# Score mask and first bias table loaded during the first value projection, half of the first pair's key copies on VectorE, the exponential's table loaded ahead

## The chip, the cores and the metric

The kernel runs on one core of a Trainium2 chip. The metric is the device time of one execution in microseconds (us). TensorE (PE) does the matrix products, VectorE (DVE), ScalarE (ACT) and GpSimd (POOL) the elementwise work, and SyncE (SP) and ScalarE issue the transfers. Each engine takes its instructions in the order in which they were put on it. A transfer issued by ScalarE stands in the same order as ScalarE's arithmetic: if its target buffer is still being read, ScalarE stands still with it.

## The reference

One step of a two-layer diffusion trunk on 512 latent tokens (a grid of 8 rows of 64) and 128 context tokens, width 1024. Only the first layer's token mixer matters here:

```python
q, k, v = jnp.split(h @ w_qkv, 3, axis=-1)          # 16 heads of 64
s_lat = einsum(qg, kg) * scale                      # each latent reads an 8 x 16 neighbourhood
bias  = rpb[:, dr, dc]                              # learned bias by relative row and column
s_lat = where(col_ok, s_lat + bias, -inf)
s_ctx = einsum(qg, k_ctx) * scale                   # and all 128 cached context keys
p = softmax(concatenate([s_lat, s_ctx]))
o = einsum(p_lat, vg) + einsum(p_ctx, v_ctx)
```

Here `h` is the RMS-normalized input, scaled and shifted by a modulation computed from the conditioning vector. The second layer (grouped-query attention) and both feed-forward blocks follow and are untouched.

## The kernel before

The kernel keeps fp32 accuracy by splitting each operand into a rounded high part (`wh`, `kh`, `hT[0]`) and a low part (`wl`, `kl`, `hT[1]`): a cast on ScalarE makes the high part, a subtraction on VectorE or GpSimd the low part, and `passes` runs three products.

The order on TensorE is written out: `mm` and `turn` chain every product and transpose to the one before. The order on the other engines is made ahead of the run by a planner: it takes the instructions in program order as priority, gives each a modelled time, and starts whatever is ready first. `behind(a, b)` adds nothing at run time; it only forces `a` after `b` in the order of their engine.

What happens around the change, in order of time:

- **First values** (lines 583 to 649). The input is normalized and transposed to `xT`. The modulation comes in four quarters: `mod_rows(i)` multiplies, ScalarE copies `row` to `rs`, `mod_cols(i)` turns it into columns, and ScalarE and VectorE write two of the eight blocks of `hT`. `normed` holds the last ScalarE and the last VectorE instruction of it. Between the quarters TensorE runs `v_part(k, ...)`, block `k` of the value projection of heads 0 to 3. Two small tables `cr` for the feed-forward convolution are loaded through ScalarE's queue and transposed on TensorE (`cp`) after `v_part(5)`. At the end `na_v_put` copies the values out of PSUM.
- **Pairs of heads.** `na_qk_items(p)` yields the work for heads 2p and 2p+1: eight parts for queries, eight for keys, each in two column halves. After a query half ScalarE and VectorE write `qs` (lines 841, 842); after a key half `k_put` (811 to 816) copies keys for both heads: for each head `b` ScalarE writes the head's own 64 partitions (814), then the same source rows into the other 64 partitions (815), and VectorE makes `kl` (816). The cached context keys go through `tk` the same way.
- **Score tables.** `na_table(h)` (883 to 896) loads runs of head h's bias into `tr` (one buffer, three transfers on ScalarE's queue, line 887) and GpSimd subtracts them from `mask` into `tb` (three instructions of 128x256, line 892). `tb` alternates between two buffers. The mask itself is loaded at line 760.
- **Heads.** `fill(PRO)` runs the first 20 parts: queries and keys of pair 0 and the first half of the queries of pair 1. Then `Head(0)` makes its table, and `scores(slot)` runs for four slots with one part (`f`) between them: two products into `s`, VectorE adds the table and takes the minimum (927), ScalarE takes the exponential (931), VectorE the reciprocal (934), GpSimd scales (935). `ORDER0` then interleaves parts, transposes `t0`..`t2` of the probabilities and the scores of the next head.

Weights come through SP's queue into four `wr` buffers well ahead of their use.

Of the kernel before, what the change touches and what calls it, by code (L numbers as in the profile page):

```python
# [10 lines left out]
F32 = mybir.dt.float32  # L11
F32R = mybir.dt.float32r
BF16 = mybir.dt.bfloat16
AF = mybir.ActivationFunctionType
# [5 lines left out]
P = 128  # L20
# [14 lines left out]
RPAD = 32  # L35
# [36 lines left out]
def raw_ap(ap, offset, dims):  # L72
    return bass.AP(tensor=ap.tensor, offset=ap.offset + offset, ap=[list(d) for d in dims])
# [30 lines left out]
def hybrid_step(ctx: ExitStack, tc: tile.TileContext, A, O):  # L104
    nc = tc.nc
# [3 lines left out]
    def pe(ins):  # L109

        if pe_last[0] is not None:
            tc.add_manual_dep(ins.ins, pe_last[0], no_sync, reason="order")
        pe_last[0] = ins.ins.name
# [3 lines left out]

    def turn(*a, **k):
        pe(nc.tensor.transpose(*a, **k))  # L119

    def f32(t):
        return t.bitcast(F32)

    def pool(name, bufs=1, side="left", **k):
        return tc.tile_pool(name=name, bufs=bufs, side=side, reuse_waits="tile", **k)
# [336 lines left out]
    hT = new_hT(r_h0.enter_context(pool("h0", 1, "right")))  # L462
    l_na = ExitStack()
    vpool = l_na.enter_context(pool("nav", 3))
    wqkv = A["na_w_qkv"][0]

    def na_v_tile():
        return vpool.tile([P, 6, 4, HD], F32, tag="vt", name="vt", bufs=2)

    def na_v_put(vt, c, src):  # L470
        nc.scalar.copy(vt[:, c], src.rearrange("p (a d) -> p a d", a=4))

    def na_v_cache(vts, g):
        vc = vpool.tile([P, 256], F32, tag="vc", name="vc", bufs=1)
# [13 lines left out]
    with ExitStack() as s:  # L488
# [57 lines left out]
        def mod_rows(i, ws):  # L546


            row = bk.get("row")
            for (n, h), w in ws.items():  # L550
                for j in range(4):
                    k = 4 * h + j
                    mm(row[32 * j : 32 * j + 32, 256 * n : 256 * n + 256], scolp[:, 2 * k : 2 * k + 32],
                       w[:, j, :], start=h == 0, stop=h == 1)
            rs = sp.tile([P, 512], F32, tag="rs", name="rs")
            nc.scalar.copy(rs, row)
            bk.put(row)
            return rs
# [46 lines left out]
        def v_part(k, cs):  # L605
            for c in cs:
                wh, wl = wv[k // 4]
                passes(vb[c][:, 0:256], tuple(x[:, k, c * P : c * P + P] for x in hT),
                       (wh[:, k % 4, :], wl[:, k % 4, :]), k == 0, k == KC - 1)
# [12 lines left out]
        mod_cols(2, rs)  # L622
        v_part(2, range(3, NT))
        v_part(3, range(NT))
        rs = mod_rows(3, loads[3])
        v_part(4, range(3))
        mod_cols(3, rs)
# [15 lines left out]
        v_part(6, range(NT))  # L643
        for c in range(NT):
            v_part(7, (c,))
            na_v_put(vts_of[0], c, vb[c][:, 0:256])
            if c == 4:
                na_v_out(0, vb[c][:, 0:256])
            bk.put(vb[c])

# [49 lines left out]
            nc.scalar.copy(hi, raw)  # L702
            return nc.vector.tensor_sub(lo, raw, f32(hi))

    def behind(ins, other):
        tc.add_manual_dep(ins.ins, other.ins.name, no_sync, reason="order")

    class Mix:


# [45 lines left out]

    with l_na:
        ap = l_na.enter_context(pool("na", 2))
        mask = ap.tile([P, 2, 32, 8], F32, name="mask", bufs=1)
        nc.scalar.dma_start(mask, A["k_mask"])  # L760
        tbs = [ap.tile([P, 7, P], F32, name=f"tb{i}", bufs=1) for i in range(2)]
        for tb in tbs:
            nc.gpsimd.memset(tb[:, 3, :], 0.0)
# [1 line left out]
        for i in range(2):  # L765
            for b in range(2):
                nc.gpsimd.memset(f32(kls[i][b])[own_oth(b)[1], :], 0.0)
        qk_of = {}

        def na_v_items(g):  # L770
            d = {}
# [25 lines left out]
        def na_qk_items(p):  # L797
            d = {}

            def load_q():  # L800
                d["w"] = wsplit(rows(wqkv, 0, 8, P * p, P), 8, P, nc.gpsimd if p else None, after=None if p else normed)
                kc = ap.tile([P, P], F32, tag="kc", name="kc", bufs=2)
                nc.scalar.dma_start(
                    kc, A["cache_na_k"][0, 0][:, 2 * p : 2 * p + 2, :].rearrange("t h d -> t (h d)")
                )
                d["kc"] = kc

            def load_k():
                d["wk"] = wsplit(rows(wqkv, 0, 8, 1024 + P * p, P), 8, P, nc.gpsimd if p else None)

            def k_put(c0, c1, src):
                for b in range(2):
                    own, oth = own_oth(b)
                    nc.scalar.copy(d["kh"][b][own, c0:c1], src[own])
                    nc.scalar.copy(d["kh"][b][oth, c0:c1], src[own])
                    nc.vector.tensor_sub(d["kl"][b][own, c0:c1], src[own], f32(d["kh"][b][own, c0:c1]))

            def part(which, half, k0):
                w = d["w"] if which == 0 else d["wk"]
                cs = QKH[half]  # L820
                nq = cs.stop - cs.start
                if k0 == 0:
                    d["ps"] = bk.get("qk")
                pp = d["ps"]
                for k in (k0, k0 + 1):
                    for n, (hx, wx) in enumerate(((0, 0), (0, 1), (1, 0))):
                        mm(pp[:, 0:nq], w[wx][:, k, :], hT[hx][:, k, cs],
                           start=k == 0 and n == 0, stop=k == 7 and n == 2)
                if k0 < 6:
                    return  # L830
                if which == 0:
                    if half == 0:
                        d["qs"] = [ap.tile([P, QW], F32R, tag=f"qs{b}", name=f"qs{b}") for b in range(2)]
                    pieces = [(slice(64 + cs.start, 64 + cs.stop), slice(0, nq))]
                    if half == 1:
                        pieces.append((slice(0, 64), slice(NS - 64 - cs.start, NS - cs.start)))
                    for qc, pc in pieces:
                        for b in range(2):
                            own, oth = own_oth(b)
                            q = d["qs"][b]  # L840
                            nc.scalar.activation(q[own, qc], pp[own, pc], AF.Copy, scale=-0.125)
                            nc.vector.scalar_tensor_tensor(
                                q[oth, qc], pp[own, pc], -0.125, f32(q[own, qc]),
                                op0=ALU.mult, op1=ALU.subtract,
                            )
                else:
                    if half == 0:
                        d["kh"] = [ap.tile([P, T + P], F32R, tag=f"kh{b}", name=f"kh{b}") for b in range(2)]
                        d["kl"] = kls[p % 2]
                        tk = bk.get("tk")  # L850
                        turn(tk[:, 0:P], d["kc"], ident)
                        k_put(CTX * P, CTX * P + P, tk[:, 0:P])
                        bk.put(tk)
                    if half == 1:
                        d["kp"] = ap.tile([P, P], F32, tag="kc", name="kp", bufs=2)
                        nc.scalar.copy(d["kp"], pp[:, NS - cs.start : T - cs.start])
                    k0 = cs.start + P * (cs.start >= CTX * P)
                    k_put(k0, k0 + nq, pp[:, 0:nq])
                    if half == 1:
                        qk_of[p] = (d["qs"], d["kh"], d["kl"])  # L860
                bk.put(pp)

            def tail():
                tk = bk.get("tk")
                turn(tk[:, 0:P], d["kp"], ident)
                ko = ap.tile([P, P], F32, tag="ko", name="ko", bufs=1)
                nc.scalar.copy(ko, tk[:, 0:P])
                bk.put(tk)
                nc.scalar.dma_start(
                    O["new_na_k"][0, 0][:, 2 * p : 2 * p + 2, :].rearrange("t h d -> t (h d)"), ko  # L870
                )

            def parts(which):
                return [(lambda h=h, k=k: part(which, h, k)) for h in range(2) for k in (0, 2, 4, 6)]

            return [(load_q, parts(0)), (load_k, parts(1))], tail
# [4 lines left out]
            return v6[:, 0:5:2, :] if slot == 0 else v6[:, slot - 1 : slot + 2, :]  # L881

        def na_table(h):
            tr = ap.tile([P, 2, RUN], F32, tag="tr", name="tr", bufs=1)
            base = h * RLEN + RPAD
            for dst, off, n in ((tr[:, 0, :], -8, 16), (tr[0:64, 1, :], 8, 8), (tr[64:128, 1, :], -16, 8)):
                nc.scalar.dma_start(dst, raw_ap(A["k_rpb"], base + off, [[1, n], [31, 8], [1, RUN]]))
            tb = tbs[h % 2]
            for w, dst in ((1, tb[:, 0::6, :]), (0, tb[:, 1:3, :]), (0, tb[:, 4:6, :])):
                t0 = tr[:, w, :]  # L890
                rv = raw_ap(t0, RUN - 1, [t0.ap[0], [-16, 2], [-1, 16], [-31, 8]])
                nc.gpsimd.tensor_sub(
                    dst.rearrange("p c (a b) -> p c a b", b=8),
                    mask[:, w].rearrange("p (c a) b -> p c a b", c=2), rv,
                )
            return tb
# [980 lines left out]
```

## Time and profile before

| what | value |
|---|---|
| median of 3 runs | 1585.63 us (1583.46 to 1588.22) |
| the profiled execution | 1584.86 us, its span 1583.0 us |
| TensorE busy | 1525.7 us (96%) |
| VectorE, ScalarE, GpSimd busy | 1022.9, 862.1, 700.9 us |
| mean granted TensorE clock | 0.988 |

The span is the time from the first to the last instruction; the execution's own time has 1.9 us more around it. "Idle before, releaser" is the time an engine stood still ahead of an instruction and what ended it. A granted clock of 1.00 is 2.4 GHz, 0.50 is 1.2 GHz. "ACTq" marks an instruction of ScalarE's sequencer, such as the issue of a transfer.

### The profile page before, as it was taken

What the parts mean: (1) busy time and instruction counts of PE and PEld (TensorE: products, weight loads), DVE (VectorE), ACT (ScalarE), POOL (GpSimd) and SP (SyncE); (2) the same over time, 40 slices, a digit from 0 to 9 for tenths busy, and PEclk for the clock granted to TensorE, in tenths of its full rate; (3) what the DMA queues carried; (4) which work ended last, traced back from release to release, by engine and by line L of the source; (5) the groups of instructions that cost most, each with busy time, mean ns of one, the idle gap of its engine ahead of it and who ended that gap; (6) DMA issues with size and microseconds to landing.
All of it is one profiled execution on the core that took longest, in us unless ns stands there. A gap on an engine that the chain in (4) does not pass through costs nothing.

```text
span 1583.0 us, 26047 instructions
## 1 busy us (share of the span) xinstructions
PE 1525.7 (96%) x9709; PEld 1351.9 (85%) x9709; DVE 1022.9 (65%) x1654; ACT 862.1 (54%) x1641; POOL 700.9 (44%) x605
## 2 busy tenths in 40 slices
PE   6899999999999999999999979999999999999998
PEld 4789899788999999988887757777899999998886
DVE  3353444549877666765746866773888888876454
ACT  4475655646655555554544436763665565665343
POOL 1455554332355455534543454542325555553333
PEclk8999999999999999999999998999999999999999
DMA  9745454244465666488563200004644333357664
GB/s 301 195 114 140 130 142 119 74 155 151 160 228 183 217 191 208 172 270 271 186 224 115 66 23 14 1 1 150 210 146 145 110 105 106 105 172 263 206 216 140
DMA packets 193210, 242.41 MB, mean 153 GB/s; under 512 B 11100, under 2 KB 149564, under 8 KB 193084
## 3 DMA queue, kind: packets, MB, share of 16 engines
q1 hardware_dynamic: 182224, 233.13, 45.4%
q10 hardware_dynamic: 10860, 7.62, 2.8%
q8 instruction: 76, 1.25, 0.3%
q14 instruction: 50, 0.41, 0.1%
HBM read 214.38 MB, written 26.34 MB: 152 GB/s over the span
## 4 chain that ended last, share of the span: by engine, by line
PE 57%; DVE 9%; POOL 5%; issue 3%; ACT 3%; DMA 1%; ACTq 0%; POOLq 0%; DVEq 0%
PE acc L116 18%; PE ux L116 16%; PE uz L116 7%; PE uy L116 4%; PE y L116 2%; PE s L116 2%; PE po L116 2%; PE tp L119 2%; PE ada L116 2%; POOL wl L1165 1%; POOL vl L1165 1%; DVE t L1241 1%; POOL rh L1485 1%; DVE al L1165 1%; DVE wl L172 1%
## 5 line engine op out<-in xcount | busy, mean ns | idle before, releaser
L172 POOL TENSOR_TENSOR wl<-wr,wh 128x1024 fp32r<-128x1024 f32 x70 | 172.6, 2467 | 235.7 <-ACT wh L170 235.4
L1165 POOL TENSOR_TENSOR wl<-wr,wh 128x1024 fp32r<-128x1024 f32 x76 | 183.6, 2438 | 45.8 <-ACT wh L1164 42.0
L116 PE MATMUL ux<-B,wh 128*128 128x322 f32 x832 | 199.8, 311 | 0.7 <-ACT u L1218 0.7
L1241 DVE SCALAR_TENSOR_TENSOR t<-C,cw,t 128x644 f32<-128x644 f32 x176 | 156.2, 887 | 52.0 <-ACT t L1239 51.4
L116 PE MATMUL acc<-wh,alo 128*128 128x512 f32 x440 | 172.3, 392 | 0.5 <-DVE alo L1134 0.5
L116 PE MATMUL acc<-wh,ahi 128*128 128x512 f32 x440 | 171.9, 391 | 0.0
L116 PE MATMUL acc<-wl,ahi 128*128 128x512 f32 x440 | 171.8, 391 | 0.0
L170 ACT CAST wh<-wr 128x1024 fp32r<-128x1024 f32 x140 | 145.1, 1047 | 37.5 <-DMA wr<-in_ffn_w_down 28.0
L116 PE MATMUL uz<-B,wh 128*128 128x322 f32 x640 | 156.2, 312 | 0.7 <-ACT v L1218 0.7
L116 PEld LDWEIGHTS ux<-B,wh 128*128 128x128 f32 x832 | 143.4, 188 | 3.1 <-ACT u L1218 0.9
L1134 DVE TENSOR_TENSOR alo<-ain,ahi 128x384 fp32r<-128x384 f32 (+1 forms) x88 | 82.3, 952 | 86.9 <-ACT ahi L1132 86.0
L116 PE MATMUL ux<-B,wl 128*128 128x322 f32 x416 | 129.2, 311 | 2.5 <-DVE wl L1165 2.5
L116 PE MATMUL qk<-hT,wh 128*128 128x384 f32 (+1 forms) x512 | 123.7, 317 | 0.0
L116 PEld LDWEIGHTS uz<-B,wh 128*128 128x128 f32 x640 | 111.1, 189 | 3.6 <-ACT vh L1164 1.2
L1165 POOL TENSOR_TENSOR vl<-wr,vh 128x1024 fp32r<-128x1024 f32 x38 | 96.1, 2528 | 24.6 <-ACT vh L1164 24.3
L1239 ACT ACTIVATE t<-C,cw 128x644 f32<-128x644 f32 x88 | 78.6, 894 | 51.1 <-DVE C L1269 42.9
L1164 ACT CAST wh<-wr 128x1024 fp32r<-128x1024 f32 x84 | 84.7, 1049 | 35.3 <-DVE wr L1188 35.0
L172 DVE TENSOR_TENSOR wl<-wr,wh 128x1024 fp32r<-128x1024 f32 x70 | 89.2, 1288 | 21.7 <-ACT wh L170 21.2
L116 PE MATMUL uz<-B,wl 128*128 128x322 f32 x320 | 99.4, 311 | 0.0
L116 PEld LDWEIGHTS acc<-wh,alo 128*128 128x128 f32 x440 | 82.5, 188 | 19.1 <-DVE alo L1134 1.4
L116 PEld LDWEIGHTS acc<-wl,ahi 128*128 128x128 f32 x440 | 82.6, 188 | 18.0
L116 PEld LDWEIGHTS acc<-wh,ahi 128*128 128x128 f32 x440 | 82.6, 188 | 17.6
(251 smaller groups left out, 3941.9 us busy)
## 6 DMA issues: line engine op xcount, KB each, us to landing
wr<-in_ffn_w_up SPq DMA_DIRECT2D x88, 512.0 KB
wr<-in_ffn_w_down SPq DMA_DIRECT2D x88, 512.0 KB
wr<-in_ada_w SPq DMA_DIRECT2D x80, 512.0 KB
act<-act SPq DMA_DIRECT2D x44, 321.0 KB
wr<-in_na_w_qkv SPq DMA_DIRECT2D x24, 512.0 KB
mod<-modrow SPq DMA_DIRECT2D x20, 512.0 KB
ain<-act SPq DMA_DIRECT2D x44, 192.0 KB
wf<-in_ada_w SPq DMA_DIRECT2D x16, 512.0 KB
```

Source lines behind the costliest of these rows:

```text
L116: pe(nc.tensor.matmul(*a, **k))
L119: pe(nc.tensor.transpose(*a, **k))
L170: i = nc.scalar.copy(hi, raw)
L172: j = (low or nc.vector).tensor_sub(lo, raw, f32(hi))
L1134: pin(nc.vector.tensor_sub(lo[:, 0 : c1 - c0], ain[:, 0 : c1 - c0], f32(hi[:, 0 : c1 - c0])))
L1164: nc.scalar.copy(hl[0], src)
L1165: low.tensor_sub(hl[1], src, f32(hl[0]))
L1239: nc.scalar.activation(t, taps(0), AF.Identity, bias=cw[:, 3, n : n + 1], scale=cw[:, 1, n : n + 1])
L1241: nc.vector.scalar_tensor_tensor(t, taps(d), cw[:, w, n : n + 1], t, op0=ALU.mult, op1=ALU.add)
L1485: last_rms[0] = nc.gpsimd.tensor_tensor(r, v, mhalf.broadcast_to([P, n]), op=ALU.pow)
```

## The change

The mask and the table runs get a pool of their own (`nat`) that exists from the start. Mask and the runs of head 0 (four transfers) are issued on ScalarE's queue behind the last ScalarE instruction of the third modulation quarter. The runs of head 1 keep their place in the program; those of head 2 are put behind the last own-half key copy of pair 0 (`kput`); later ones are as before. For pair 0 alone, VectorE makes the copies into the other 64 partitions (six instructions) instead of ScalarE. A one-column exponential after the last copy of the first values makes ScalarE load that function's table there.

```diff
+    tpool = l_na.enter_context(pool("nat"))
+    mask = tpool.tile([P, 2, 32, 8], F32, name="mask")
+    runs = {}
+
+    def na_runs(h, after=None):
+        tr = runs[h] = tpool.tile([P, 2, RUN], F32, tag="tr", name="tr", bufs=1)
+        base = h * RLEN + RPAD
+        for dst, off, n in ((tr[:, 0, :], -8, 16), (tr[0:64, 1, :], 8, 8), (tr[64:128, 1, :], -16, 8)):
+            i = nc.scalar.dma_start(dst, raw_ap(A["k_rpb"], base + off, [[1, n], [31, 8], [1, RUN]]))
+            if after:
+                behind(i, after)
...
         v_part(3, range(NT))
+        behind(nc.scalar.dma_start(mask, A["k_mask"]), normed[0])
+        na_runs(0, normed[0])
         rs = mod_rows(3, loads[3])
...
-            na_v_put(vts_of[0], c, vb[c][:, 0:256])
+            i = na_v_put(vts_of[0], c, vb[c][:, 0:256])
...
+        behind(nc.scalar.activation(sm.tile([P, 1], F32, name="exp1"), mhalf, AF.Exp), i)
...
-        mask = ap.tile([P, 2, 32, 8], F32, name="mask", bufs=1)
-        nc.scalar.dma_start(mask, A["k_mask"])
...
-                    nc.scalar.copy(d["kh"][b][own, c0:c1], src[own])
-                    nc.scalar.copy(d["kh"][b][oth, c0:c1], src[own])
+                    i = nc.scalar.copy(d["kh"][b][own, c0:c1], src[own])
+                    (nc.scalar.copy if p else nc.vector.tensor_copy)(d["kh"][b][oth, c0:c1], src[own])
                     nc.vector.tensor_sub(d["kl"][b][own, c0:c1], src[own], f32(d["kh"][b][own, c0:c1]))
+                if not p:
+                    kput[:] = [i]
...
-            tr = ap.tile([P, 2, RUN], F32, tag="tr", name="tr", bufs=1)
-            base = h * RLEN + RPAD
-            for dst, off, n in ((tr[:, 0, :], -8, 16), (tr[0:64, 1, :], 8, 8), (tr[64:128, 1, :], -16, 8)):
-                nc.scalar.dma_start(dst, raw_ap(A["k_rpb"], base + off, [[1, n], [31, 8], [1, RUN]]))
+            if h:
+                na_runs(h, kput[0] if h == 2 else None)
+            tr = runs.pop(h)
```

## Rows read from the trace of the kernel before

**Rows 1.** What TensorE waited for between 40 and 84 us: total, times, longest.

```profile
PE s L116 <- ACT kh L815: 7.4, 1, 7.4
```

**Rows 2.** Windows: busy us of PE, PEld, DVE, ACT, POOL; granted clock, DMA share, GB/s.

```profile
43.00:50.00 7.00, 7.00 (x76) 5.80 (x74) 4.14 (x11) 3.36 (x8) 0.00 (x0) 1.00 1.18 292
...
71.50:78.90 7.40, 0.05 (x1) 0.05 (x1) 1.72 (x6) 4.00 (x14) 2.66 (x4) 0.67 0.69 113
...
78.85:84.44 5.59, 5.59 (x18) 5.20 (x19) 2.88 (x8) 5.45 (x11) 3.79 (x3) 0.52 0.27 63
84.44:89.00 4.56, 4.56 (x32) 4.50 (x31) 2.57 (x9) 2.69 (x7) 3.31 (x5) 1.00 0.32 95
...
130.00:373.00 243.00, 240.47 (x1684) 210.53 (x1681) 118.60 (x300) 137.42 (x360) 108.06 (x128) 1.00 0.45 130
```

**Rows 3.** Timeline of PE, 68 to 86 us: start, duration, instruction, idle before.

```profile
68.25 0.45 PE L116 MATMUL qk<-hT,wh 128*128 128x384 f32 x2
...
71.16 0.28 PE L116 MATMUL qk<-hT,wh 128*128 128x256 f32 x1
78.85 0.69 PE L116 MATMUL s<-kh,qs 128*128 128x384 f32 x1 [7.40 <-ACT kh L815]
...
84.44 0.33 PE L116 MATMUL s<-kh,qs 128*128 128x384 f32 x1
...
85.84 0.34 PE L116 MATMUL s<-kh,qs 128*128 128x384 f32 x1
```

**Rows 4.** Timeline of ACT, 60 to 83 us.

```profile
60.73 2.04 ACTq L887 DMA_DIRECT2D tr<-in_k_rpb  x3
...
69.32 1.24 ACTq L887 DMA_DIRECT2D tr<-in_k_rpb  x2
70.61 0.22 ACT L841 ACTIVATE qs<-qk 64x64 fp32r<-64x64 f32 x1 [5.36 <-issue]
...
75.80 1.84 ACTq L887 DMA_DIRECT2D tr<-in_k_rpb  x3
77.68 0.27 ACT L856 COPY kp<-qk 128x128 f32<-128x128 f32 x1 [3.23 <-issue]
77.84 0.47 ACT L814 CAST kh<-qk 64x384 fp32r<-64x384 f32 x1
...
81.27 1.28 ACT L931 ACT_TABLE_LOAD   x1
```

**Rows 5.** Timeline of POOL, 58 to 76 us.

```profile
58.60 2.39 POOL L172 TENSOR_TENSOR wl<-wr,wh 128x1024 fp32r<-128x1024 f32 x1
66.21 1.70 POOL L892 TENSOR_TENSOR tb<-mask,tr 128x256 f32<-128x256 f32 x2 [5.22 <-DMA tr<-in_k_rpb]
68.42 0.87 POOL L892 TENSOR_TENSOR tb<-mask,tr 128x256 f32<-128x256 f32 x1 [0.50 <-DMA tr<-in_k_rpb]
...
72.74 1.66 POOL L892 TENSOR_TENSOR tb<-mask,tr 128x256 f32<-128x256 f32 x2 [1.09 <-DMA tr<-in_k_rpb]
```

**Rows 6.** Timeline of DVE: one copy out of PSUM.

```profile
91.92 0.69 DVE L946 COPY pk<-tp 128x512 f32<-128x512 f32 x1
```

**Rows 7.** Timeline of ACT, 41 to 58 us.

```profile
41.27 0.57 ACTq L633 DMA_DIRECT2D cr<-in_ffn_conv_w  x1
...
43.08 0.48 ACT L578 ACTIVATE hT<-xT,hcol,gcol 128x128 fp32r<-128x128 f32 x1
45.42 0.59 ACT L556 COPY rs<-row 128x512 f32<-128x512 f32 x1 [1.86 <-PE row L116]
...
54.35 0.36 ACTq L760 DMA_DIRECT2D mask<-in_k_mask  x1
...
57.20 0.38 ACT L841 ACTIVATE qs<-qk 64x256 fp32r<-64x256 f32 x1 [2.22 <-PE qk L116]
```

**Rows 8.** Timeline of PE, 46 to 50 us.

```profile
46.41 0.95 PE L116 MATMUL col<-sel,rs 128*128 128x2 f32 x8
...
49.89 0.69 PE L119 MATMUL cp<-ident,cr 44*128 44x44 f32 x8
```

More of the change, by code (lines that the diff above doesn't have):

```diff
@@ L119, in turn, with behind @@
         pe(nc.tensor.transpose(*a, **k))
+    def behind(ins, other):
+        tc.add_manual_dep(ins.ins, other.ins.name, no_sync, reason="order")
     def f32(t):
@@ L470, in na_v_put @@
     def na_v_put(vt, c, src):
-        nc.scalar.copy(vt[:, c], src.rearrange("p (a d) -> p a d", a=4))
+        return nc.scalar.copy(vt[:, c], src.rearrange("p (a d) -> p a d", a=4))
     def na_v_cache(vts, g):
@@ L703, in split @@
             return nc.vector.tensor_sub(lo, raw, f32(hi))
-    def behind(ins, other):
-        tc.add_manual_dep(ins.ins, other.ins.name, no_sync, reason="order")
     class Mix:
@@ L767, in hybrid_step @@
                 nc.gpsimd.memset(f32(kls[i][b])[own_oth(b)[1], :], 0.0)
-        qk_of = {}
+        qk_of, kput = {}, []
         def na_v_items(g):
```

## Prediction

> **What bounds the kernel now.** I read the waits of TensorE first, because it is busy for 240.5 of 243 us in a later stretch [rows 2]: what is worth anything here is time in which TensorE stands still or runs slowly. Between 40 and 84 us it has one wait on the list, 7.4 us ahead of the first scores `s`, and the releaser is a key copy on ScalarE [rows 1]. TensorE's own timeline shows the place: the last product of the prologue starts at 71.16 and ends at 71.44, and the first score product starts at 78.85 [rows 3]. The keys that the scores need were multiplied by 68.70 [rows 3], so ScalarE had 2.7 us to copy them and took more than 10.
>
> ScalarE's timeline says why, and it is not arithmetic. Over the 7.4 us it was busy for 4.0 [rows 2]. It stood still for 5.36 us up to 70.61 and again for 3.23 us up to 77.68, both times behind an issue of `tr` transfers [rows 4]. There is one `tr` buffer: the loads for head 1 (69.32) wait until GpSimd has read head 0's runs, the loads for head 2 (75.80) until it has read head 1's, and the key copies stand behind them in ScalarE's order. GpSimd was not slow either: it idled 5.22 us for head 0's runs to land, since they were issued only at 60.73 and the first subtraction started at 66.21, the third at 68.42 [rows 4, 5]. So the chain is: runs issued late, table late, next runs' issue blocked, keys late, TensorE idle.
>
> The stall costs a second time. From 78.85 to 84.44 the granted clock averages 0.52, that is the 1.2 GHz level, after it had been 1.00 before and fell while TensorE idled; from 84.44 on it is 1.00 again [rows 2].
>
> **The change part by part.**
>
> *The stall.* With the runs and the mask on their way by about 45 us, GpSimd can make head 0's table long before 66 us. Its earliest and latest place by these rows: after the transfers have landed, or, if the planner puts it behind every weight split of the prologue, after 60.99 (58.60 + 2.39), then three subtractions of 0.87, so done by 63.6 [rows 5]. The issue for head 1 then stands in ScalarE's order at 63.6 at the latest instead of 69.32, and that for head 2 may not come before the last own key copy. ScalarE's work after the last key product at 68.70 is `kp` 0.27, then two own copies of 0.47 [rows 4]: 69.9 with nothing in between. VectorE's two copies into the other half: its copy of 512 columns out of PSUM takes 0.69 [rows 6]; 0.69 is therefore the upper end for 384 columns and three quarters of it (0.52) the lower. Two of them and two `kl` subtractions of at most 0.69 make 2.8 us if all four count, 71.5; for head 0 only the first copy and the first subtraction do, 70.1. Both are about when TensorE arrives (71.44). VectorE was busy 1.7 us of the 7.4 [rows 2], so these six copies lie in idle time; if that cover were gone, they would cost at most 6 x 0.69 = 4.1 us in all, no more than the same copies cost on ScalarE plus a quarter. I take the whole 7.40 as gone, and 0.2 us back for a late subtraction.
>
> *The slow clock.* From the third score product (84.44) to the fourth (85.84) TensorE does one slot and one part in 1.40 us at 1.00. From 78.85 to 84.44 it does two slots and two parts, and it needs 5.59 [rows 3]. At 2.4 GHz that is 2.80, so 2.8 us more are saved, 2.7 without the one small transpose in it. Below a full removal: if a stall of a few us remains, so may this term; the ends are 0 and 2.8, and I take 2.7.
>
> *Issuing four transfers earlier.* They come behind the activation that starts at 43.08 and ahead of the copy `rs` that starts at 45.42 after 1.86 us of idle time [rows 7]. The mask's issue took 0.36 [rows 7] and three `tr` issues 2.04 [rows 4], 2.40 together. An issue can run beside an activation still in flight, so they end between 45.5 and 46.0 (43.08 or 43.56 + 2.40). `rs` then ends at 46.1 to 46.6 against TensorE's use at 46.41 [rows 8]: 0 to 0.2 us of cost, 0.1 taken. The same 2.40 us disappear later, from between 54.35 and 69.32, where ScalarE mostly waits.
>
> *The table load.* It took 1.28 us at 81.27 [rows 4], between a slot's minimum and its exponential, with TensorE busy on parts beside it: worth nothing by itself. At its new place about 55 us ScalarE has 2.22 us of idle time before 57.20 [rows 7]; the mask's issue goes from there too, so 1.28 and a one-column activation fit. If that cover were gone, `qs` would be 1.5 us later, and it is needed only 14 us afterwards.
>
> *What is late next.* With TensorE at full clock and no stall, the first transposes `t0` come earlier, and they need all four probability tiles: minimum, exponential, reciprocal and scaling after the fourth score product. The pace of one slot per 1.40 us is the one that the other engines already kept from 84.44 on [rows 3]; GpSimd's 3.31 us busy of 4.56 there [rows 2] leaves little room for a stray 2.39 us weight split [rows 5]. The bounds are 0 and 2.4; the row from 84.44 to 89.00 without a PE wait is the nearest, so I take 0.3.
>
> **Sum.** 7.40 + 2.70 - 0.2 - 0.1 - 0.3 = 9.5 us. After that TensorE is the bound with almost no idle time (2.5 us of 243) and nothing there waits on a fixed time, so the gain passes on to the end. Against the profiled execution's 1584.86 this is 1575.4; the median shown, 1585.63, stands 0.8 above it, so I forecast 1576.0, its own range 1573.5 to 1578.5.
>
> **The rivals.**
>
> *Half a stall.* The planner counts the landing of runs shorter than it is, which is how the `tr` issues came to block in the trace: head 0's runs took 5.5 us from issue to first use, head 1's 3.4 (69.32 to 72.74) [rows 4, 5]. In the change the issue for head 1 carries no `behind`. If it is held by GpSimd to about 66, ScalarE has the query pieces, a weight cast and all of the first key half behind it, and keys are ready some 2 to 5 us after 71.44. With the clock falling again in the upper half of that, the gain is 2 to 7: 1579 to 1583.6. For it: the single `tr` buffer stays. Against: the late end worked out above is 63.6.
>
> *The change does not do it.* The wait moves to head 2's issue or to GpSimd and the stall stays near 7 us: 1585.
>
> *The transfers collide.* From 43 to 50 us the DMA engines are at a share of 1.18 and 292 GB/s [rows 2]. The mask is 128 x 512 x 4 bytes and the runs 128 x 498 x 4, together 0.52 MB, which at that rate is 1.8 us. If the next weights or `hT` wait for it, 1.8 us come back: 1577.8. Against: TensorE needs no new weights before the first query products, and the loads are ahead of use. The Trainium skill, "DMA: Bandwidth & Descriptors", section "Issuing engines are not separate DMA queues", says that transfers issued by different engines run on the same 16 DMA engines and interleave; by that rule the early loads do slow the weights, against this change.
>
> *Slower.* One mechanism: the `cr` loads. TensorE transposes `cr` at 49.89 [rows 8], and they were issued at 41.27 [rows 7], through the same ScalarE queue. If mask and runs are put ahead of them, `cr` lands later by 1.8 us at the full rate, or, at the pace of head 0's runs (60.73 to 68.42 for half as many bytes), by up to 15. It decides when it passes the 10 us gained: 13 us of stall and some 5 us of slow clock after it against 10 gives about 1593. Against: the `cr` issues run from 41.27, before the activation that the new loads are put behind.
>
> **How the numbers follow.** The forecast 0.66; half a stall 0.15; no effect 0.08; the collision 0.06; slower 0.05. A time is told from no change by about 0.3% (4.8 us; the three runs span as much). Faster, below 1580.9: the forecast, the collision and under half of the half stall, 0.79. Same: the rest of it and no effect, 0.16. Slower 0.05. The range 1572.5 to 1581.5 holds the forecast with the spread of its bounds, the collision and half of the half stall.
>
> **What would show it.** Right: head 0's table finished before 64 us; key copies of pair 0's second half starting within 0.5 us of 68.7; the first score product at 71.4 to 72.0; granted clock 1.00 from 70 to 85; `rs`, `col` and `cp` within 0.3 us of their places; the table load near 55. Wrong: ScalarE idle in front of a `tr` issue after 64 us, TensorE waiting at `s`, at `t0` for GpSimd, or at `cp` for `cr`; or a gain of 10 us at 90 us that has shrunk by 370.

## The result and the profile after

The change gained nothing: the median is 1587.97 us against 1584.95 of the kernel before on the same chips, a ratio of 1.0017 with a 95% interval of 1.0011 to 1.0023. That is 3.0 us slower, inside the 0.3% that the prediction called no change, and 12 us from its forecast. The profiled execution has a span of 1586.9 us.

Three rows of TensorE's waits over the whole span, of the kernel after (total, times, longest); the row of before, from 40 to 84 us, is [rows 1]:

```profile
PE col L116 <- ACT rs L571: 2.4, 2, 1.7
PE s L116 <- DVE kh L828: 2.0, 1, 2.0
PE tp L119 <- POOL p L949: 1.9, 2, 1.1
```

The stall at `s` has gone from 7.4 to 2.0, as it was meant to. Two waits are new: 1.71 us at `col` for `rs`, and 1.05 us at the transposes `tp` for GpSimd's probabilities, at 87.50 (the rest of these two rows, 0.7 and 0.9 us, lies elsewhere and before has it too). Windows of the kernel after (the columns of [rows 2]):

```profile
43.00:54.00 11.00, 9.29 (x57) 8.51 (x50) 3.28 (x10) 5.71 (x8) 0.00 (x0) 0.69 0.95 275
71.50:78.90 7.40, 5.30 (x33) 4.84 (x32) 5.59 (x15) 4.42 (x12) 5.59 (x3) 0.89 0.35 98
78.90:84.40 5.50, 5.50 (x29) 5.41 (x28) 3.51 (x13) 2.78 (x9) 1.76 (x3) 0.84 0.85 160
```

From 78.9 to 84.4 the granted clock is 0.84 where it was 0.52. But from 43 to 54 it is 0.69, while before had 1.00 from 43 to 50 [rows 2]. TensorE and GpSimd there, after:

```profile
42.74 0.64 PE L116 MATMUL row<-wf,scolp 128*32 128x256 f32 x8 [0.87 <-DMA wf<-in_ada_w]
...
46.35 1.76 PE L116 MATMUL col<-sel,rs 128*128 128x2 f32 x8 [1.71 <-ACT rs L571]
...
52.73 0.93 PE L119 MATMUL cp<-ident,cr 44*128 44x44 f32 x8
...
76.50 0.45 PE L116 MATMUL s<-kh,qs 128*128 128x384 f32 x1 [1.96 <-DVE kh L828]
...
87.50 0.33 PE L119 MATMUL tp<-ident,p 128*128 128x128 f32 x1 [1.05 <-POOL p L949]
```
```profile
60.80 2.54 POOL L906 TENSOR_TENSOR tb<-mask,tr 128x256 f32<-128x256 f32 x3
```

Head 0's table is done at 63.34, where the prediction put it (63.6). ScalarE's timeline of the kernel after says what is late instead:

```profile
38.27 0.82 ACT L593 ACTIVATE hT<-xT,hcol,gcol 128x512 fp32r<-128x512 f32 x1 [0.60 <-DVE gcol L587]
38.28 0.34 ACTq L640 DMA_DIRECT2D mask<-in_k_mask  x1
...
41.23 1.36 ACTq L650 DMA_DIRECT2D cr<-in_ffn_conv_w  x1
42.64 0.39 ACTq L651 DMA_DIRECT2D cr<-in_ffn_conv_b  x1
45.31 0.31 ACTq L650 DMA_DIRECT2D cr<-in_ffn_conv_w  x1
45.72 0.59 ACT L571 COPY rs<-row 128x512 f32<-128x512 f32 x1 [5.15 <-DMA tr<-in_k_rpb]
...
65.33 0.46 ACTq L490 DMA_DIRECT2D vc<-in_cache_na_v  x1
...
71.78 0.41 ACT L486 COPY vt<-vc 128x256 f32<-128x256 f32 x1 [4.00 <-DMA vc<-in_cache_na_v]
72.33 0.35 ACT L827 CAST kh<-qk 64x256 fp32r<-64x256 f32 x1
```

Two things are to be seen. At 38 us the four new issues stand in front of the `cr` issues, and the copy `rs` stands behind the third of these, seen at 45.31, although the product that it copies was ready at 43.38 (42.74 + 0.64, above). At 72 us the key copies stand behind a copy of cached values that waits 4.00 us for its load.

A table by stage compares kernels better than single times do. It runs from ScalarE's first `hT` activation of the third modulation quarter to the first `cp`, the first `s`, the fourth score product, the first `ux` (the feed-forward block) and the end of the span, each read from the timeline of its profile, in us:

| kernel | hT at | to cp | to s | to 4th s | to ux | to the end | span |
|---|---|---|---|---|---|---|---|
| before | 41.26 | 8.63 | 28.96 | 6.99 | 286.04 | 1211.1 | 1583.0 |
| after | 38.27 | 14.46 | 23.77 | 6.39 | 287.66 | 1216.4 | 1586.9 |
| after minus before | -2.99 | +5.83 | -5.19 | -0.60 | +1.62 | +5.3 | +3.9 |

Up to `hT` no instruction of the change has run. Kernels with before's order had their `hT` at 38.25 to 38.45 in three other profiles (e3, e7, e14 below), so the first column is the scatter of single executions: from 28 to 36 us the granted clock is 0.50 in before's profile, and 1.00 in these three and in after's. These three are therefore the better measure for the next columns. In them `hT` to `cp` took 9.59 to 9.71 us, with a wait of 0.78 to 0.90 us for `wf`, the modulation's weights, that after has as well (0.87), `cp` to `s` 29.24 to 30.25 and the four score products 6.18 to 6.79. Against them the change loses 4.8 us ahead of `cp` and wins 5.5 to 6.5 at `s`. So what it won up to the fourth score product it had all but lost ahead of `cp`, and another 6.9 us went after that. The late loss has its own row, here the products with the high activations in the last block (tile `acc`: shortest, median and longest ns, first and last start), first of the kernel before, then after:

```profile
L116 PE MATMUL acc<-wh,ahi x220: 387/389/399, 1425.2 to 1575.8; 128*128 128x512 f32 x110
```
```profile
L116 PE MATMUL acc<-wh,ahi x220: 387/393/404, 1426.6 to 1579.8; 128*128 128x512 f32 x110
```

The same products on the same tiles take 393 ns in the median instead of 389, 1.3 ms after the change. That the prediction had not considered at all.

### The profile page after: what moved, and what is told of

Read it like the earlier page. It is cut to its first block, busy times and chain, and to the rows that moved or that the text cites. A ratio compares the mean times of both kernels' runs of the same rounds, so it can differ in the third digit from the quotient of the medians.

```text
span 1586.9 us, 26053 instructions
## 1 busy us (share of the span) xinstructions
PE 1533.0 (97%) x9709; PEld 1352.6 (85%) x9709; DVE 1020.7 (64%) x1660; ACT 860.8 (54%) x1636; POOL 701.1 (44%) x605
## 4 chain that ended last, share of the span: by engine, by line
PE 54%; DVE 10%; POOL 5%; issue 3%; ACT 3%; DMA 1%; ACTq 0%; POOLq 0%; DVEq 0%
PE acc L116 18%; PE ux L116 15%; PE uz L116 6%; PE uy L116 4%; PE y L116 2%; PE s L116 2%; PE po L116 2%; PE tp L119 2%; PE ada L116 2%; POOL wl L1179 1%; DVE t L1255 1%; DVE al L1179 1%; POOL vl L1179 1%; POOL rh L1499 1%; DVE wl L175 1%
## 5 line engine op out<-in xcount | busy, mean ns | idle before, releaser
L1148 DVE TENSOR_TENSOR alo<-ain,ahi 128x384 fp32r<-128x384 f32 (+1 forms) x88 | 77.4, 896 | 94.1 <-ACT ahi L1146 93.8
```

The lines of the kernel that those rows point to most:

```text
L1148: pin(nc.vector.tensor_sub(lo[:, 0 : c1 - c0], ain[:, 0 : c1 - c0], f32(hi[:, 0 : c1 - c0])))
```

## The experiments

Ratios are to the kernel before, with 95% intervals; "us" are medians.

**e1: the exponential's one-column tile elsewhere.** The changed kernel allocates `exp1` in the long-lived pool `sm` (four slots of 32 bytes), which moves every buffer laid out behind it by 128 bytes. Here it is in a pool that is gone before the late stages.

```diff
-        behind(nc.scalar.activation(sm.tile([P, 1], F32, name="exp1"), mhalf, AF.Exp), i)
+        behind(nc.scalar.activation(sp.tile([P, 1], F32, name="exp1"), mhalf, AF.Exp), i)
```

> The changed kernel with the one-column output of the early exponential put into the pool of the first stage in place of the small long-lived pool, so that nothing allocated after that pool moves by 128 bytes. Theory A (the move of the later buffers slows the products of the last stage): between 1430 and 1510 us the products come as often as in the kernel before (about 353 in 80 us in place of 345), and the time falls by about 3 us to 1585. Theory B (the loss is all in the first 60 us, from transfers that the early loads delay): the products of the last stage stay at 345 in 80 us and the time stays at 1588.

Measured: 1582.26 us, 0.9976 (0.9966 to 0.9986). From `ux` to the end it takes 1213.6 us instead of 1216.4. The edit is not the shift alone: from about 48 us on the planner orders loads, and then copies, another way, and the wait at `s` is 1.10 us instead of 1.96. But the shift shows earlier as well, in the loads of `wf`, before any instruction of the change has run and with the same order of loads. The window from 28 to 36 us (last two numbers: share of the DMA engines, GB/s) of after, then of e1:

```profile
28.00:36.00 8.00, 7.52 (x80) 5.71 (x73) 5.37 (x13) 2.98 (x6) 0.00 (x0) 1.00 1.10 349
```
```profile
28.00:36.00 8.00, 7.96 (x83) 6.90 (x83) 4.60 (x11) 3.81 (x6) 0.00 (x0) 1.00 1.09 384
```

The last of these loads lands at 42.70 in after and at 39.67 in e1. All seventeen profiles fall into these two groups: 347 to 349 GB/s with before's allocation, shifted or not, and with the changed one with the shift (before, after, e2, e3, e4, e7, e8, e14), and 381 to 385 with the changed one without it (e1, e5, e6, e9 to e13, e15).

**e2: the four loads later.** Mask and head 0's runs are issued behind the fourth modulation quarter, so behind the `cr` issues and `rs`.

```diff
-        behind(nc.scalar.dma_start(mask, A["k_mask"]), normed[0])
-        na_runs(0, normed[0])
         rs = mod_rows(3, loads[3])
         v_part(4, range(3))
         mod_cols(3, rs)
+        behind(nc.scalar.dma_start(mask, A["k_mask"]), normed[0])
+        na_runs(0, normed[0])
```

> The changed kernel with mask and first runs issued one modulation quarter later, after the last hT activations. Theory A: the time is that of the changed kernel within 1 us, since the late stage is untouched. Theory B (the small convolution tables wait for the mask's landing, and the copy rs behind them): no idle time of ScalarE in front of the fourth rs copy, the column product without its wait of 1.7 us and no half clock at 46 to 53 us; 3 to 5 us less, 1584. Half-stall rival: the first score product still waits 2 to 4 us.

Measured: 1580.98 us, 0.9971 (0.9961 to 0.9982). `hT` to `cp` is 8.63 as before, `cp` to `s` 21.41, and there is no wait at `s`.

**e3, e7, e14: the kernel before with nothing but a shift.** A one-column tile in `sm`, written once at the start, moves the buffers behind it; its slots make it 128 bytes (e3), 256 (e7, `bufs=8`) or 64 (e14, `bufs=2`). The order on every engine is that of before, apart from this write.

```diff
     nc.gpsimd.memset(scolp, 0.0)
+    nc.gpsimd.memset(sm.tile([P, 1], F32, name="pad"), 0.0)
```

> The kernel before with one more one-column buffer in the small long-lived pool (four slots, 128 bytes) that one memset at the start writes; nothing else differs. Theory A: about 3 us slower than the kernel before, 1588, all of it after 1070 us, with 345 products in 80 us of the last stage. Theory B: the time of the kernel before within 1 us.

Measured: 1588.61 us, 1.0023 (1.0014 to 1.0032).

> The kernel before with 256 bytes in front of the later buffers in place of 128. If any move slows the products of the last stage, about 345 in 80 us from 1430 on; if what counts is the place within 256 bytes, 356 as in the kernel before; if it is within 512 bytes or more, slower again.

Measured: 1585.01 us in one execution.

> The kernel before with 64 bytes in front of the later buffers. If only a place on a multiple of 256 bytes is fast, about 345 products in 80 us from 1430 on, as with 128; if 64 bytes is a step that does not matter, 356.

Measured: 1586.46 us in one execution. The windows from 1470 to 1510 us (first number in brackets: products of TensorE in 40 us) of before, e3 and e14:

```profile
1470.00:1510.00 40.00, 40.00 (x178) 33.14 (x177) 18.73 (x17) 14.52 (x23) 15.68 (x9) 1.00 0.56 186
```
```profile
1470.00:1510.00 40.00, 40.00 (x174) 32.44 (x173) 15.15 (x16) 15.43 (x23) 15.72 (x9) 1.00 0.61 191
```
```profile
1470.00:1510.00 40.00, 40.00 (x173) 32.25 (x172) 18.67 (x17) 14.51 (x23) 16.48 (x9) 1.00 0.57 182
```

TensorE is busy all the time at a clock of 1.00 in all three, and with a shift of 128 or 64 bytes it gets through 174 or 173 products instead of 178. With 256 bytes it is 178 again, in the same window of e7:

```profile
1470.00:1510.00 40.00, 40.00 (x178) 33.14 (x177) 16.53 (x17) 14.27 (x22) 15.62 (x9) 1.00 0.56 186
```

From `ux` to the end before takes 1211.1 us, e7 1211.6, e14 1214.8, e3 1216.8.

**e4: the cached values behind the keys.** In the changed kernel, the copy that waited 4.00 us is put behind pair 0's last own key copy.

```diff
-        na_v_put(vts, 5, vc)
+        i = na_v_put(vts, 5, vc)
+        if g == 1:
+            behind(i, kput[0])
```

> The changed kernel with the copy of the second group's cached values put behind the key copies of pair 0. Theory: the 4.0 us in which ScalarE waits for that load to land no longer stand in front of the key copies, the wait of 2.0 us at the first score product goes, and with it 2 to 3 us: 1585. Rival (the key copies are late for another reason, the weight cast or the issue of the next runs): the wait at the first score product stays above 1.5 us and the time at 1588.

Measured: 1586.41 us, 1.0003 (0.9994 to 1.0012). The wait at `s` is gone, but TensorE waits afterwards: the fourth score product to `ux` takes 290.83 instead of 287.66.

**e5 and e6: the repairs together.** e5 is e1 and e2 in one; e6 adds e4.

> Both repairs together: mask and first runs issued after the last hT activations, and the early exponential's output in the pool of the first stage. If the two costs are independent, the late loads give 7.0 us against the changed kernel and the place of the output some 3 us in the late stages: 1578, 7 us faster than the kernel before, with 353 products in 80 us from 1430 on. If instead the gain of the one run with the late loads already contains the other, 1581.

> The same with the copy of the second group's cached values put behind the key copies of pair 0. If that copy still stands in front of the keys, 1 to 2 us less than without (1576 to 1577). Rival: with the late loads the first score product already starts without a wait, so nothing is left to win there: the same time within 1 us.

Measured: e5 1576.75 us, 0.9952 (0.9940 to 0.9965); e6 1579.34, 0.9967 (0.9955 to 0.9979). In e5 the planner orders the copies another way and nothing waits at `s`, so e4's edit has nothing to repair. Why e6 comes out 2.6 us above e5 these runs do not show; the intervals overlap. What e5 still waits for, in TensorE's and GpSimd's timelines and the window behind them:

```profile
66.98 0.45 PE L116 MATMUL s<-kh,qs 128*128 128x384 f32 x1
...
76.92 0.33 PE L119 MATMUL tp<-ident,p 128*128 128x128 f32 x1 [1.96 <-POOL p L949]
...
78.86 0.47 PE L119 MATMUL tp<-ident,p 128*128 128x128 f32 x1 [1.05 <-POOL p L949]
```
```profile
74.63 1.66 POOL L906 TENSOR_TENSOR tb<-mask,tr 128x256 f32<-128x256 f32 x2 [2.34 <-DMA tr<-in_k_rpb]
76.28 1.15 POOL L949 TENSOR_SCALAR p<-p,rc 128x384 f32<-128x384 f32 x2
...
78.22 0.58 POOL L949 TENSOR_SCALAR p<-p,rc 128x384 f32<-128x384 f32 x1
```
```profile
78.00:85.00 7.00, 6.14 (x26) 6.04 (x27) 2.80 (x10) 2.95 (x10) 4.26 (x5) 0.52 0.45 102
```

GpSimd stands 2.34 us in front of head 2's table, which nobody needs yet, and head 0's probability scalings stand behind it; TensorE waits at `t0`, and the clock falls to 0.52 for the next 7 us.

**e8: only VectorE's key copies, in the kernel before.**

```diff
-                    nc.scalar.copy(d["kh"][b][oth, c0:c1], src[own])
+                    (nc.scalar.copy if p else nc.vector.tensor_copy)(d["kh"][b][oth, c0:c1], src[own])
```

> The kernel before with VectorE making pair 0's copies into the other half, and nothing else of the change. By the chain told for the kernel before (ScalarE held in front of the runs' issues) the first score product still waits 5 to 7 us: 1 to 2 us faster, 1583.5. Rival: the copies themselves were the cost; the wait falls under 3 us and with it the slow clock: 1578.

Measured: 1586.84 us, 1.0013 (1.0004 to 1.0022); the wait at `s` is 8.3 us, and in the four profiles with before's order it is 7.4 to 8.7.

**e9 and e10: tables behind the probabilities.** e5, and head 2's three subtractions come behind head 0's last scaling in GpSimd's order; in e10 every head h above 1 comes behind head h - 2.

```diff
+                i = nc.gpsimd.tensor_sub(...)
+                if h == 2:
+                    behind(i, scaled[h - 2])
...
+                scaled[self.h] = nc.gpsimd.tensor_scalar(
```

> The kernel with both repairs, and head 2's three table subtractions put behind the last probability scaling of head 0 on GpSimd. Theory: in the repaired kernel TensorE stands still for 4.1 us in front of the first transposes because GpSimd, in its order, waits 2.3 us for head 2's runs to land and makes two tables before the last scaling; that goes, and the half clock after it (6.8 us at half speed, 3.4 us lost) too: 1576.8 to 1570. Rival (the scalings are late because minimum and exponential are): the wait stays above 2 us and the time at 1576.

> The same for every later head's table, not head 2's alone. If GpSimd is held by runs that land late at every head, 1 to 3 us less than with head 2 alone; if only the first has no work to cover it, the same time within 1 us.

Measured: e9 1574.54 us, 0.9933 (0.9921 to 0.9945), the fastest version found; e10 1590.12, 1.0029 (1.0019 to 1.0039). GpSimd's and TensorE's timelines of e9:

```profile
76.66 0.58 POOL L951 TENSOR_SCALAR p<-p,rc 128x384 f32<-128x384 f32 x1 [0.90 <-DVE rc L950]
77.20 2.52 POOL L906 TENSOR_TENSOR tb<-mask,tr 128x256 f32<-128x256 f32 x3
```
```profile
77.30 0.33 PE L119 MATMUL tp<-ident,p 128*128 128x128 f32 x1 [0.82 <-POOL p L951]
```

The last scaling now stands ahead of the table, `t0` waits 0.82 us once, and the clock from 72 to 85 us is 1.00. In e10 the old mechanism comes back for the later heads: the tables free the one `tr` buffer later, the next issue of runs blocks ScalarE, and its query and key copies are late. The waits of TensorE, then of ScalarE, from 84 to 400 us in e10:

```profile
PE po L116 <- DVE qs L857: 5.2, 3, 1.7
PE tp L119 <- DVE kl L829: 3.8, 3, 1.3
PE s L116 <- DVE qs L857: 2.6, 3, 0.9
```
```profile
ACT kp L871 <- DMA tr<-in_k_rpb: 16.3, 3, 5.4
ACT vt L486 <- DMA tr<-in_k_rpb: 14.8, 3, 4.9
```

In e9 ScalarE has no wait behind `tr` among the longest of that stretch.

**e11, e12, e15: the other two parts, each left out.** e11 is e5 without the early exponential; e12 is e5 with ScalarE's key copies; e15 is e9 without either.

> The kernel with both repairs, without the early exponential (so also without its buffer): the function table is loaded in front of the first exponential again. Theory: 1.28 us on ScalarE with TensorE busy on other parts, no effect within 1 us: 1577. Rival: the first probabilities are the next thing that TensorE waits for, so 1 to 1.5 us more and more slow clock: 1578 to 1580.

> The kernel with both repairs, with pair 0's copies into the other half on ScalarE as in the kernel before. Theory: ScalarE has the six copies (2.2 us) more, with 1.2 us to spare before the first score product: a wait of about 1 us there and 1 to 2 us more: 1578. Rival: they are hidden, 1576.8 within 1 us.

> The repaired kernel with head 2's table behind the scalings, without the early exponential and without VectorE's copies: only the loads of mask and first runs are moved. Theory: the two other edits are worth nothing, 1574.5 within 1.5 us. Rival: without them the planner's order again puts the wait for the cached values in front of the key copies and the copies fill ScalarE, a wait of 1 to 2 us at the first score product: 1577.

Measured: e11 1576.64 us, 0.9944 (0.9931 to 0.9957); e12 1575.50, 0.9938 (0.9926 to 0.9951); e15 1576.07, 0.9952 (0.9937 to 0.9966). The intervals of e11 and e12 overlap that of e5, and those of e15 and e9 overlap too: neither part has a value that these runs can tell from nothing, though up to 3 us for both together (0.0019 between the ratios of e9 and e15) is not excluded. With the earlier loads alone the stall is gone: in e15 TensorE does not wait at `s`.

**e13: the loads early, but `cr` behind `rs`.** e1, and the four `cr` issues stand behind the copy that they had held up. If only the place of `rs` were wrong, this would be as good as e5.

```diff
-            nc.scalar.copy(rs, row)
+            rowed[:] = [nc.scalar.copy(rs, row)]
...
-            nc.scalar.dma_start(cr[:, 0:3, :], ...)
+            behind(nc.scalar.dma_start(cr[:, 0:3, :], ...), rowed[0])
-            nc.scalar.dma_start(cr[:, 3, :], ...)
+            behind(nc.scalar.dma_start(cr[:, 3, :], ...), rowed[0])
```

> The changed kernel without the move of 128 bytes, with the early loads where they are and the four loads of the convolution tables put behind the fourth rs copy. Theory (order: rs stood behind an issue that waits for the mask to land): rs starts when its row product ends, the column product has no wait above 0.8 us, and the time comes within 2 us of the kernel with both repairs: 1577 to 1579. Rival (contention: half a megabyte more in the busiest 10 us delays weights and modulation rows whatever the order): the time stays with the early loads' 1582.

Measured: 1583.52 us, 0.9993 (0.9985 to 1.0002), no better than e1. ScalarE's and TensorE's timelines of e13:

```profile
42.36 0.58 ACT L571 COPY rs<-row 128x512 f32<-128x512 f32 x1 [1.84 <-PE row L116]
42.38 0.34 ACTq L650 DMA_DIRECT2D cr<-in_ffn_conv_w  x1
44.44 0.31 ACTq L651 DMA_DIRECT2D cr<-in_ffn_conv_b  x1
...
45.26 0.38 ACTq L651 DMA_DIRECT2D cr<-in_ffn_conv_b  x1
```
```profile
47.16 0.78 PE L119 MATMUL cp<-ident,cr 44*128 44x44 f32 x7 [0.26 <-DMA cr<-in_ffn_conv_w]
48.81 0.25 PE L119 MATMUL cp<-ident,cr 44*128 44x44 f32 x1 [0.88 <-DMA cr<-in_ffn_conv_b]
```

`rs` waits only for its product, as before, but `cr` now lands late: TensorE waits 1.14 us at `cp`, and `cp` to `s` takes 25.33 us instead of e5's 21.51. The early place costs in this order too.

The stages of the kernels that decide, as in the table above:

| kernel | hT at | to cp | to s | to 4th s | to ux | to the end | median |
|---|---|---|---|---|---|---|---|
| e1 | 36.86 | 11.64 | 23.59 | 4.91 | 289.25 | 1213.6 | 1582.26 |
| e2 | 41.23 | 8.63 | 21.41 | 4.41 | 289.12 | 1215.0 | 1580.98 |
| e5 | 36.48 | 8.99 | 21.51 | 4.86 | 292.32 | 1212.4 | 1576.75 |
| e9 | 38.16 | 8.61 | 21.53 | 4.84 | 287.97 | 1212.1 | 1574.54 |
| e13 | 38.22 | 8.94 | 25.33 | 4.90 | 291.11 | 1212.0 | 1583.52 |

## Why the prediction was wrong

**The stall and the slow clock: right in mechanism and size.** The sum took 7.40 us at `s` and 2.70 us of clock. Where nothing else disturbs it (e2, whose `hT` is as late as before's), `cp` to `s` is 28.96 - 21.41 = 7.55 us shorter than before and the four score products 6.99 - 4.41 = 2.58 shorter; the first of them starts at 71.27, where the prediction said 71.4 to 72.0. In the changed kernel itself 1.96 us of the stall stayed, since the cached values' load was issued only at 65.33, behind head 1's runs, and its copy stood ahead of the keys; the prediction looked for nothing in that place but table loads. It mattered little: without it (e4) the four score products take 4.34 us instead of 6.39, but 3.2 us more pass up to `ux`, and the median fell by 1.6 us.

**The failed step: "Against: the `cr` issues run from 41.27, before the activation that the new loads are put behind."** This put the rival "Slower" at 0.05, and the 0.1 us for the four issues rests on it. It took the time of an issue for its place. The instructions of ScalarE in the order of the built program (after; the name in brackets is the counter whose earlier transfer an issue waits for, and which it then uses itself):

```
30 L593 ACTIVATE hT_122<-xT,hcol,gcol 128x128
31 L640 DMA mask<-in_k_mask 128x512 [waits DMAHW5_49]
32 L476 DMA tr<-in_k_rpb 128x1x249 [waits DMAHW6_49]
33 L476 DMA tr<-in_k_rpb 64x1x249 [waits DMAHW7_49]
34 L476 DMA tr<-in_k_rpb 64x1x249 [waits DMAHW1_49]
35 L650 DMA cr<-in_ffn_conv_w 44x3x128 [waits DMAHW2_49]
36 L651 DMA cr<-in_ffn_conv_b 44x128 [waits DMAHW3_49]
37 L650 DMA cr<-in_ffn_conv_w 44x3x128 [waits DMAHW5_49]
38 L571 COPY rs<-row 128x512 [waits PE_49,Activation_49]
```

`cr` stands behind all four activations of the quarter, in before too. It was seen at 41.27 although the last of these activations started only at 43.08 [rows 7]: ScalarE's sequencer had gone on to the issues. So the new loads, put behind the last activation, came ahead of `cr` and not behind it. The second `cr` weight issue then takes the counter that the mask uses, and waits for the mask to land: that is the 2.28 us from 43.03 (42.64 + 0.39) to 45.31, with `rs` behind it. (The timeline names the runs, issued just behind the mask, as what ended the wait. The trace's records of landings settle it: the last part of the mask landed at 45.29, 0.02 us before the issue.) The loss up to `cp` comes apart at the timeline's marks, counted from `hT` in each kernel, against e3, e7 and e14 with their equally early `hT`: `row` ends at +5.11, in those at +5.01 to +5.12; `col` starts at +8.08 instead of +6.11 to +6.23, 1.9 us, behind `rs`; and from `col` to `cp` it is 6.38 us instead of 3.48, another 2.9, at a clock that fell while TensorE waited (0.69 on average from 43 to 54). e2 takes the loads away from there and has before's 8.63 back.

e13 takes `rs` out of that wait, but not `cr`: the second `cr` issue again uses the mask's counter and stands from 42.72 (42.38 + 0.34) to 44.44, and the mask landed at 44.41. `cr` then lands 1.14 us too late for TensorE, followed by a slow clock. The prediction had put its rival as `cr` landing late by the pace of the transfer, at a price of 13 us. Here it is late by its issue: the edit alone starts the issues 4.2 us behind `hT` (in before at once), and the last `cr` transfer took 3.5 us from issue to landing (45.26 to 48.76), in the kernel before 6.6 (42.64 to 49.22). What e13 would give with a counter of its own for the mask was not tried, so how much of the loss the order explains alone stays open.

The rival of colliding transfers got nothing from TensorE's waits: the 0.87 us that `row` waited for `wf` stand in e3, e7 and e14 too, without the early loads. The transfers did share, however: weights issued at 36.62 landed at 46.20 in the changed kernel, and at 44.67 in e3 (issued at 36.60), but TensorE did not wait for them. The Trainium skill, "DMA: Bandwidth & Descriptors", section "Issuing engines are not separate DMA queues", says that transfers of different issuers interleave on the same engines; these landings agree with it.

**The omitted term: where the buffers lie.** The one-column output of the early exponential, priced as a 1.28 us table load in idle time, moved later buffers by 128 bytes. Alone (e3) that costs 3.5 us by the medians, 5.7 from `ux` to the end by the profiles, with no order changed; e5 beats e2 by 0.0019 in ratio, 3.0 us, when the shift goes in addition. e1 beats the changed kernel by more, 5.7 us. Part of that is the planner's other order. Part is a second cost of the shift in the changed kernel: the first loads run at 349 GB/s with it and at 384 without, and the fourth `row` ends at 40.87 in e1 instead of 43.38. The prediction had neither. In the built programs `wf` lies on a multiple of 256 bytes in exactly the nine kernels with the faster loads; no run moved `wf` alone, so that this is the reason is not shown.

**The under-sized term: `t0`.** The prediction named the place, GpSimd's probabilities, gave it bounds of 0 and 2.4 us and took 0.3. From the fourth score product to `ux`, e2 gives back 3.1 us, e5 6.3 and the changed kernel 1.6. In the stretch from which 0.3 was taken [rows 2], GpSimd made head 2's table between the scalings too, but from 82.28 us on and without a wait: its runs, issued at 75.80 [rows 4], had landed. With the stall gone the scalings come up some 12 us earlier and head 2's runs are issued from 68.35 in e5, so GpSimd reaches that table before its data: the 2.34 us are what the old stall had hidden. Ordering that one table (e9) gives 4.4 of the 6.3 back in the profile, and the medians of e5 and e9 differ by 2.2 us.

**The table load and VectorE's copies.** The load was priced at nothing, and e11 agrees. The copies were counted as part of what takes the stall away; e12 and e15 lose nothing that their intervals can tell without them, and e8 gains nothing with them alone. The loads do it. (The prediction's aside that six copies of 0.69 us cost no more than ScalarE's plus a quarter does not add up: six of 0.47 are 2.8 us, and 4.1 is half as much again. Nothing hangs on it.)

**The whole.** Repaired at its place and without the shift (e5), the change gives 7.8 us against the 9.5 forecast, by its ratio 7.6; with e9's order it gives 10.9. That these come near the forecast is partly luck. They hold the faster first loads, which the prediction did not know of: the fourth `row` ends at 40.87 in e5 and at 42.17 in e9, and at 43.27 to 43.57 in e3, e7 and e14, so by these profiles some 1.1 to 2.7 us of the gain come from there. Open stays why products slow down with a shift, and why loads speed up without it.

## What to carry to other kernels

The time at which an issue is seen tells nothing of its place in its engine's order: before putting a load "behind" an instruction, write down what stands between the two in program order, and what the next issues on that queue will wait for. When a wait goes, look at who else is on the engine that fed it, because the next piece of work that was too late to be in the way now arrives in time to be so. And if a change makes a late and untouched stage slower with no engine waiting, undo its allocations before its instructions; an early stretch of loads can show the same, in its GB/s.

## What the runs showed of the hardware

- Moving buffers by 64 or 128 bytes, with the same instructions in the same order, made products of 512 columns slower in the last block: 178 to 173 or 174 in 40 us, and with 128 bytes 393 ns in the median instead of 389, at a granted clock of 1.00. A move of 256 bytes did not. It depends on the stage: from 690 to 770 us, `acc` products of the first layer's block, TensorE did 358 in 80 us both before and after.
- A shift of 128 bytes between two kernels with the same order of loads up to there (after and e1) changed the pace of the first loads: 349 GB/s with it and 384 without, from 28 to 36 us, at DMA shares of 1.10 and 1.09.
- An issue of a transfer stood for 2.28 us on ScalarE because an earlier transfer on the same counter had not landed: that one landed at 45.29, the issue came at 45.31, and the copy behind it started 2.34 us after its product was ready. In e13 the same pair is 44.41 and 44.44.
- The time of an issue is not its place in the order: `cr` was issued at 41.27, and an activation ahead of it in ScalarE's order started at 43.08 [rows 7].
